# Row statistics of a hybrid attention/LRU layer: spread over partitions by two DMAs instead of two products

## The chip, the cores and the metric

The kernel runs on one core of one Trainium2 chip. The metric is the device time of one execution in microseconds (us). In the rows below PE is TensorE (PEld its weight loads), DVE VectorE, ACT ScalarE, POOL GpSimd, and SP the engine that does nothing here but issue DMAs. A name such as `SPq` is an engine's queue of issued instructions.

## The reference

One layer of a trunk over 512 tokens of width 2048: a norm, one input projection, an attention group and a recurrent (LRU) group side by side, a norm and a gate for each group, one output projection.

```python
h = rms_norm(x, norm_w)
proj = jnp.einsum('bsd,de->bse', h, w_in)
q, k, v, g_attn, xr, g_lru = jnp.split(proj, SPLITS, axis=-1)
attn_out = attention_group(q, k, v, q_norm_w, k_norm_w)
lru_out = lru_group(xr, conv_w, conv_b, lru_wa, lru_ba, lru_wx, lru_bx, lru_lambda)
mixed = jnp.concatenate([rms_norm(attn_out, attn_norm_w) * jax.nn.silu(g_attn),
                         rms_norm(lru_out, lru_norm_w) * jax.nn.silu(g_lru)], axis=-1)
return x + jnp.einsum('bse,ed->bsd', mixed, w_out)
```

`rms_norm` divides a token's row by the root of its mean square and multiplies by a weight for each column. Everything is float32.

## The kernel before

**Layout.** Activations are held with features on the 128 partitions and the 512 tokens along the free axis. Each float32 operand of a product is split into a high part in the matmul's input format (fp32r) and a low part, the rest; a product is then three matmuls (`mm3`, L153 to L155). The high part is made on ACT (`wh`, L218), the low part on DVE (`wl`, L219), so every 512 KB chunk of weights passes a DMA (`wr`, L206, a ring of three buffers), two ACT casts and two DVE subtractions before PE can use it.

**The norm's weights.** `norm_w` scales the features of x. It is loaded as 16 rows of 128 (`nw_st`), turned to a column per 128 features by a PE product with the identity (`columns`, L189) and copied to `nw` by DVE (L191). `xturn` (L253 to L261) turns a block of x on PE, scales it by a column of `nw` into the high part (ACT, L258) and the low part (DVE, L261).

**A row's statistic.** The mean square of a token's row is not applied to x, but to what comes out of the projections, where a token is a place on the free axis. So its reciprocal root, computed as one number per token on the partitions (a 128 x 4 tile), must stand on all 128 partitions along the free axis (128 x 512). `rows` does that: it splits the column into high and low part (L354, L355), spreads each over a diagonal matrix of 128 x 512 (L357), multiplies both by a matrix of ones on PE (L363) and copies the result from PSUM (L364). It is used three times: for `rbc`, the statistic of x, in `xstats`; for `gbc`, that of the LRU group, at the end of `kv`; for `gbc` again, that of the attention group, in `later`.

**The stages around the change.** First the LRU input is projected (`proj_feat(C_XR, ...)`, eight chunks of x and weights); its PSUM banks are emptied by DVE with a product by `rbc` (`evac_bc`, L466). Then come the second half of it with the LRU itself, k and v, the two halves of q, and the gates with the attention. `kv` runs beside the projection of q: POOL raises the LRU group's mean squares to the power of -0.5 (`rsqrt_mean`, L343 and L344, tile `r_l`), four fill steps later `rows` makes `gbc`, and `normed` (L826) multiplies the four pairs of LRU outputs `hs` by it on DVE. When q's second half is done, ACT empties its banks (L591), and `norm_rope` normalises and rotates it on DVE (L608 to L617) with statistics `rr` from POOL. The first head's q, which went through DRAM to be turned (`put_aside`, `bring_back`, tiles `qd` and `lq`, L289 and L296), is split into parts by ACT and DVE (L648) and enters the first product with k.

**What sets the order.** PE runs in the order in which the program is written. ACT, DVE and POOL are ordered by a scheduler from priorities, except at the very start and at the end. SP's issues are in written order during the first projection and in the attention, and the scheduler's between. Each engine runs its own list strictly in order: an instruction that waits holds up all behind it. SP and ACT issue DMAs into queues over the same 16 DMA engines; each of these DMAs takes one of eight semaphores in turn, and waits for the landing of the DMA that had it before. POOL also issues DMAs that add rows of `w_out` into DRAM (`t`, L897).

`moves` is a table that says at which step of the first projection a chunk's next stage is written: `x5` is the next stage of x's chunk 5 (load, turn in 32 x 32 blocks, put aside in DRAM, bring back, split), `w5` and `s5` load and split the weights of chunk 5.

Of the kernel before, what the change touches and what calls it, by code (L numbers as in the profile page):

```python
# [17 lines left out]
P = 128  # L18
# [21 lines left out]
SOON = 150  # L40


WARM, WARM2 = 11, 5


BEGIN, STEPS, LATE = 11, 2, 3
# [17 lines left out]
def hybrid_kernel(  # L64
# [53 lines left out]
    def nm(s):  # L118
        cnt[0] += 1
        return f"{s}_{cnt[0]}"  # L120
# [4 lines left out]
    def k2(dt=F32, shape=(P, SEQ)):  # L125
        return pools["lru"].tile(list(shape), dt, tag="k2", bufs=LRU_K2, name=nm("k2"))
# [19 lines left out]
    def const(shape, name, dt=F32):  # L146
        return cp.tile(list(shape), dt, tag=name, name=name)

    def f(ap):
        return ap.bitcast(F32)  # L150
# [29 lines left out]
            nc.sync.dma_start(vec_st[lo : lo + src.shape[0], :], src)  # L180

    nw = const([P, KT], "nw")
    vec = const([P, R_END], "vec")

    def columns(dst, src):

        n = src.shape[0]
        pt = mm()
        nc.tensor.transpose(pt[:, :n], src, ident[:n, :n])  # L189
        with tc.high_priority():  # L190
            nc.vector.tensor_copy(dst, pt[:, :n])  # L191
# [8 lines left out]
    def wraw(w, r0, c0, nk=1, queue=nc.sync):  # L200

        raw = wring.tile([P, 2, SEQ], F32, name=nm("wr"))
        src = w[r0 : r0 + 2 * P, c0 : c0 + SEQ].rearrange("(k p) e -> p k e", p=P)
        for k in range(nk):
            ks = slice(k * 2 // nk, (k + 1) * 2 // nk)
            loads_done[queue] = queue.dma_start(raw[:, ks, :], src[:, ks, :]).ins  # L206
            yield raw
# [26 lines left out]
    def xload(c, nk=1):  # L234

        xc = b4(shape=(P, NT, 2 * P))
        for k in range(nk):
            ks = slice(k * 2 * P // nk, (k + 1) * 2 * P // nk)
            cs = slice(c * 2 * P + ks.start, c * 2 * P + ks.stop)
            nc.sync.dma_start(xc[:, :, ks], xf[:, cs].rearrange("(t p) d -> p t d", p=P))  # L240
            yield xc
# [7 lines left out]
    def xturn(xc, kk, then=None):  # L249
        pt = mm()  # L250
        for t in range(NT):
            ks = slice(kk % 2 * P, (kk % 2 + 1) * P)
            nc.tensor.transpose(pt[:, t * P : (t + 1) * P], xc[:, t, ks], ident)  # L253
        if then:
            then()
        xh[kk], xl[kk] = x2(), x2()
        with behind(split_done[-1] if kk > 3 else ()):
            highs[kk // 2] = nc.scalar.activation(  # L258
                xh[kk], pt, AF.Identity, scale=nw[:, kk : kk + 1]
            ).ins  # L260
        nc.vector.scalar_tensor_tensor(  # L261
            xl[kk], pt, nw[:, kk : kk + 1], f(xh[kk]), op0=ALU.mult, op1=ALU.subtract
        )

    def xsquare(xc, c):
# [83 lines left out]
    def rows(dst, col, dg):  # L349

        shape = [P, NT, P]
        part = [const([P, NT], nm("part")) for _ in range(2)]
        parts = [dg() for _ in part]
        nc.vector.tensor_copy(part[0].bitcast(F32R), col)  # L354
        nc.vector.tensor_sub(part[1], col, part[0])  # L355
        for c, d in zip(part, parts):
            nc.vector.tensor_mul(  # L357
                d, ident[:, None, :].broadcast_to(shape), c[:, :, None].broadcast_to(shape)
            )
        pb = mm()  # L360
        for k, d in enumerate(parts):
            d = d.rearrange("p t q -> p (t q)")
            nc.tensor.matmul(pb, ones_r, d, start=k == 0, stop=k == 1)  # L363
        nc.vector.tensor_copy(dst, pb)  # L364

    def xstats():
        s = const([P, NT], "xsum")
        nc.vector.reduce_sum(s, ssq, axis=AX.X)
        rsqrt_mean(rstd, s, DM, NT)
        rows(rbc, rstd, lambda: k2(F32R, (P, NT, P)))  # L370

# [278 lines left out]
    def kv(es):  # L650
        turned_k = sent(norm_rope(es, NKV, rk), NKV)
        yield 20
        opened("wx", "right")
        for t in range(NT):
            vv = es[t][:, NKV * HD :]
            vt = aside(
                lambda *a: pools["qkv"].tile(*a, tag="v", bufs=NT, name=nm("v")), 2 * NKV * HD // H
            )
            vh[t], vl[t] = vt[:, 0, :], vt[:, 1, :]
            nc.scalar.copy(vh[t], vv)  # L660
            nc.vector.tensor_sub(vl[t], vv, f(vh[t]))
        yield from lru_squares()
        yield 2
        drain(turned_k)
        yield 6
        pair = landed(asides.pop(0))
        for h in range(NKV):
            yield (12, 4)[h]
            kt = pools["qkv"].tile([P, 2, SEQ], F32R, tag="kt", bufs=NKV, name=nm("kt"))
            kth[h], ktl[h] = kt[:, 0, :], kt[:, 1, :]  # L670
            split_head(pair, h, kth[h], ktl[h])
        r = group_rstd(sums["l"], "r_l", NB * P)
        yield 4
        rows(
            gbc, r,
            lambda: pools["rope"].tile([P, NT, P], F32R, tag="kv", bufs=NT, name=nm("kv")),
        )

    qs = {}

# [468 lines left out]
    given = {}  # L1149
    with tc.high_priority():  # L1150
        xs, ws = xload(0, 2), wraw(w_in, 0, C_XR, 2)
        nc.scalar.dma_start(nw_st, norm_w.rearrange("(k p) -> k p", p=P))
        xc, raw = next(xs), next(ws)
        next(xs), next(ws)
        table = const([P, 1], "table")
        nc.scalar.activation(table, ones[:, :1], AF.Exp)
        first = []

        def scales():
            columns(nw, nw_st)  # L1160
            first.append(wsplit(raw, 0, nc.vector.tensor_copy))

        xturn(xc, 0, scales)
        busy(WARM2)
    chunks = [xchunk(c) for c in range(1, KT // 2)]

    raws = {}
# [5 lines left out]
    def split_x(c):  # L1173
# [10 lines left out]
    }  # L1184

    def move(step):
        for name in moves.get(step, "").split():
            n = int(name[1])
            if name[0] == "x":
                next(chunks[n - 1])  # L1190
            else:
                (fetch_x if name[0] == "w" else split_x)(n)

    for step in proj_feat(C_XR, a1, first, given):
        if step is None:
            with tc.high_priority():
                first.append(wsplit(raw, 1))
                xturn(xc, 1)
            xsquare(xc, 0)
            move(None)  # L1200
            given[1] = wload(w_in, 2 * P, C_XR)
            continue
        c, e = step
        move(step)
        if (c, e) == (1, 2):
            s2.close()
        if (c, e) == (4, 2):
            with tc.high_priority(AHEAD):
                vec_load()
        if (c, e) == (7, 1):  # L1210
            columns(vec, vec_st)
        if (c, e) == (KT // 2 - 1, 0):
            with tc.high_priority(), tc.issue_after(x_parts[1]):
                xstats()

    s1.close()
    last_x = loads_done["lru"] = loads_done[nc.sync]
# [213 lines left out]
```

## Time and profile before

| | us |
|---|---|
| time, median of 3 runs | 631.48 (631.18 to 632.32) |
| the profiled execution's own time | 631.68 |
| its span, first to last instruction | 629.9 |
| PE busy in the span | 624.1 (99%) |
| DVE busy | 491.5 (78%) |
| ACT busy | 348.3 (55%) |
| POOL busy | 103.6 (16%) |

Times in rows are from the span's start. What lies outside the span is 1.8 us of the profiled execution. PE is busy almost throughout, so what changes the time is what PE executes, and the places where it waits for another engine's result.

### The profile page before, as it was taken

The numbers are of one execution on the slowest core, as the hardware profiler recorded it, in microseconds if no ns is written. First come the engines' busy times: TensorE is split into PE (matmuls) and PEld (weight loads), VectorE is DVE, ScalarE is ACT, GpSimd is POOL, SyncE is SP. The second block draws the span as 40 slices with busy tenths as digits, with TensorE's granted clock in tenths as the row PEclk, the third lists the DMA queues.
The fourth block names the chain that finished last, engine by engine and source line by source line (L and its number), as shares of the span: only waits on it lengthen the run. The fifth ranks groups of instructions, "written<-read, shape, count | busy, mean of one in ns | idle before, by whom it ended". The sixth has DMA issues, their size and how long they took to land.

```text
span 629.9 us, 8298 instructions
## 1 busy us (share of the span) xinstructions
PE 624.1 (99%) x2768; PEld 514.0 (82%) x2768; DVE 491.5 (78%) x796; ACT 348.3 (55%) x612; POOL 103.6 (16%) x137
## 2 busy tenths in 40 slices
PE   9999999999999999999999999999999999999997
PEld 7887888888888888888888888888888888888885
DVE  5948879986699874887887888549978866886875
ACT  3764799479945812555475447435445633444441
POOL 0001110112003631622122232100300001010010
PEclk9999999999999999999999999999999999999999
DMA  9878785859784599479669646923995677896262
GB/s 292 279 208 248 185 206 148 183 138 199 232 233 135 170 250 232 99 208 270 186 175 250 201 146 188 267 69 129 254 223 187 210 253 237 293 330 223 68 200 100
DMA packets 73594, 127.61 MB, mean 203 GB/s; under 512 B 6616, under 2 KB 29264, under 8 KB 73552
## 3 DMA queue, kind: packets, MB, share of 16 engines
q1 hardware_dynamic: 65664, 109.65, 56.4%
q0 software_dynamic: 7712, 17.31, 14.3%
q8 instruction: 21, 0.34, 0.2%
q14 instruction: 21, 0.17, 0.1%
q10 hardware_dynamic: 176, 0.14, 0.1%
HBM read 110.29 MB, written 37.75 MB: 235 GB/s over the span
## 4 chain that ended last, share of the span: by engine, by line
PE 95%; DMA 2%; DVE 1%; SPq 1%; ACT 0%; issue 0%; POOL 0%; DVEq 0%; ACTq 0%; POOLq 0%
PE pj L153 19%; PE pj L155 19%; PE pj L154 19%; PE mm L1021 14%; PE pj L1021 10%; PE mm L155 4%; PE mm L153 3%; PE mm L154 3%; PE pj L383 1%; DMA xd<-xu 1%; DMA xu<-xd 1%; PE mm L253 1%; PE mm L1139 1%; SPq L296 0%; DVE xu L281 0%
## 5 line engine op out<-in xcount | busy, mean ns | idle before, releaser
L153 PE MATMUL pj<-x,wh 128*128 128x512 f32 x376 | 146.9, 391 | 0.0
L154 PE MATMUL pj<-x,wh 128*128 128x512 f32 x376 | 146.5, 390 | 0.0
L155 PE MATMUL pj<-x,wl 128*128 128x512 f32 x376 | 146.5, 390 | 0.0
L218 ACT CAST wh<-wr 128x512 fp32r<-128x512 f32 x143 | 85.7, 618 | 93.0 <-PE pj L154 36.3
L219 DVE TENSOR_TENSOR wl<-wr,wh 128x512 fp32r<-128x512 f32 x144 | 100.2, 723 | 18.7 <-ACT wh L218 17.5
L873 ACT CAST wh<-wr 128x1024 fp32r<-128x1024 f32 (+1 forms) x72 | 60.7, 860 | 75.0 <-PE mm L1021 35.4
L874 DVE TENSOR_TENSOR wl<-wr,wh 128x1024 fp32r<-128x1024 f32 (+1 forms) x72 | 68.7, 985 | 29.7 <-ACT wh L873 29.6
L155 PEld LDWEIGHTS pj<-x,wl 128*128 128x128 f32 x376 | 70.6, 188 | 15.2 <-DVE wl L219 0.3
L154 PEld LDWEIGHTS pj<-x,wh 128*128 128x128 f32 x376 | 70.6, 188 | 14.6
L153 PEld LDWEIGHTS pj<-x,wh 128*128 128x128 f32 x376 | 70.6, 188 | 14.6
L153 PE MATMUL pj<-wh,x 128*128 128x512 f32 x192 | 74.8, 390 | 0.0
L155 PE MATMUL pj<-wh,x 128*128 128x512 f32 x192 | 74.7, 389 | 0.0
L154 PE MATMUL pj<-wl,x 128*128 128x512 f32 x192 | 74.7, 389 | 0.0
L897 POOL DMA_DIRECT2D t<-in_w_out_dram x40 | 33.7, 914 | 131.7 <-DMA t<-in_w_out_dram 88.4
L1021 PE MATMUL mm<-wl,mh 128*128 128x512 f32 x128 | 49.8, 389 | 0.0
L1021 PE MATMUL mm<-wh,mh 128*128 128x512 f32 x128 | 49.8, 389 | 0.0
L1021 PE MATMUL mm<-wh,ml 128*128 128x512 f32 x128 | 49.8, 389 | 0.0
L154 PEld LDWEIGHTS pj<-wl,x 128*128 128x128 f32 x192 | 36.0, 188 | 7.5
L153 PEld LDWEIGHTS pj<-wh,x 128*128 128x128 f32 x192 | 36.0, 188 | 7.5
L155 PEld LDWEIGHTS pj<-wh,x 128*128 128x128 f32 x192 | 36.0, 188 | 7.5
L703 POOL TENSOR_SCALAR p<-p,sm 128x512 f32<-128x512 f32 x32 | 23.7, 744 | 89.8 <-DVE sm L702 89.8
L1021 PE MATMUL pj<-wl,mh 128*128 128x512 f32 x96 | 37.4, 390 | 0.0
(209 smaller groups left out, 1035.5 us busy)
## 6 DMA issues: line engine op xcount, KB each, us to landing
wr<-in_w_in_dram SPq DMA_DIRECT2D x71, 512.0 KB, 5.1
wr<-in_w_out_dram SPq DMA_DIRECT2D x24, 512.0 KB, 5.2
t<-in_w_out_dram POOLq DMA_DIRECT2D x40, 256.0 KB, 7.0
wr<-t SPq DMA_DIRECT2D x40, 256.0 KB, 6.0
pd<-u SPq DMA_DIRECT2D x16, 512.0 KB, 3.0
pt<-pd SPq DMA_DIRECT2D x64, 128.0 KB, 3.8
t<-in_w_out_dram SPq DMA_DIRECT2D x24, 256.0 KB, 5.3
t<-t SPq DMA_DIRECT2D x16, 256.0 KB, 5.2
```

What stands on the lines that cost most here:

```text
L153: nc.tensor.matmul(acc, lh, rh, start=start, stop=False)
L154: nc.tensor.matmul(acc, lh, rl, start=False, stop=False)
L155: nc.tensor.matmul(acc, ll, rh, start=False, stop=stop)
L218: copy(hi, raw[:, k, :]).ins,
L219: nc.vector.tensor_sub(lo, raw[:, k, :], f(hi)).ins,
L253: nc.tensor.transpose(pt[:, t * P : (t + 1) * P], xc[:, t, ks], ident)
L383: nc.tensor.matmul(acc[e], w[:, e * P : (e + 1) * P], x_[k], start=k == 0 and j == 0, stop=False,)
L703: last_pool[0] = nc.gpsimd.tensor_scalar(p, p, sm, 0.0, op0=ALU.mult, op1=ALU.add).ins
L873: nc.scalar.copy(hi[:, to], b)
L874: nc.vector.tensor_sub(lo[:, to], b, f(hi[:, to]))
L897: nc.gpsimd.dma_start(dst, src, accum_op=ALU.add)
L1021: nc.tensor.matmul(dst[s], lh[:, ts_], rh, start=i == 0 and j == 0, stop=i == 7 and j == 2)
```

## The change

`spread` takes the place of `rows` for `rbc` and for the LRU group's `gbc`: SP writes the 128 x 4 column to 512 consecutive floats in DRAM (`line`), waits until that has landed, and reads them back to all 128 partitions at once. The attention group keeps `rows`. `xstats` becomes a generator with two stages, written at two places of the `moves` table (`t0`), in place of a call behind the last split of x. The first two columns of the norm's weights are fetched by a DMA of their own, issued by ACT, straight into `nw0`; the turn of all 16 columns stays, but is written behind the second block of x. Of the small products that keep PE busy while it waits for the first data (`busy`), the second batch is three instead of five.

```diff
-WARM, WARM2 = 11, 5
+WARM, WARM2 = 11, 3
...
+    nw0 = const([P, 2], "nw0")
+
+    def scale_of(kk):
+        return (nw if kk > 1 else nw0)[:, kk : kk + 1]
...
-                xh[kk], pt, AF.Identity, scale=nw[:, kk : kk + 1]
+                xh[kk], pt, AF.Identity, scale=scale_of(kk)
...
-            xl[kk], pt, nw[:, kk : kk + 1], f(xh[kk]), op0=ALU.mult, op1=ALU.subtract
+            xl[kk], pt, scale_of(kk), f(xh[kk]), op0=ALU.mult, op1=ALU.subtract
...
+    def spread(dst, col):
+
+        line = dram.tile([SEQ], F32, name=nm("line"), tag="line", bufs=2)
+        nc.sync.dma_start(line.rearrange("(t p) -> p t", p=P), col)
+        yield
+        nc.sync.dma_start(dst, line[None, :].broadcast_to([P, SEQ]))
+        yield
+
     def xstats():
         s = const([P, NT], "xsum")
         nc.vector.reduce_sum(s, ssq, axis=AX.X)
         rsqrt_mean(rstd, s, DM, NT)
-        rows(rbc, rstd, lambda: k2(F32R, (P, NT, P)))
+        yield from spread(rbc, rstd)
...
         r = group_rstd(sums["l"], "r_l", NB * P)
         yield 4
-        rows(
-            gbc, r,
-            lambda: pools["rope"].tile([P, NT, P], F32R, tag="kv", bufs=NT, name=nm("kv")),
-        )
+        drain(spread(gbc, r))
...
+        nc.scalar.dma_start(nw0, norm_w[: 2 * P].rearrange("(k p) -> p k", p=P))
         nc.scalar.dma_start(nw_st, norm_w.rearrange("(k p) -> k p", p=P))
...
-        def scales():
-            columns(nw, nw_st)
-            first.append(wsplit(raw, 0, nc.vector.tensor_copy))
-
-        xturn(xc, 0, scales)
+        xturn(xc, 0, lambda: first.append(wsplit(raw, 0, nc.vector.tensor_copy)))
         busy(WARM2)
+    stats = xstats()
...
-        (4, 0): "x6 w7 x7", (4, 3): "s5 x6",
+        (4, 0): "x6 t0 w7 x7 t0", (4, 3): "s5 x6",
...
+            elif name[0] == "t":
+                with tc.high_priority(AHEAD):
+                    next(stats)
...
                 xturn(xc, 1)
+                columns(nw, nw_st)
...
-        if (c, e) == (KT // 2 - 1, 0):
-            with tc.high_priority(), tc.issue_after(x_parts[1]):
-                xstats()
```

How the built programs stand, at the three places that matter. The first is SP's list in the first projection, where chunk 6 of x is brought back (`xu`), the weights of chunk 7 are loaded and chunk 7 is brought back; the two `xd` ahead are the writes that put them aside. Before:

```order
L289 DMA xd_437<-xu_425 128x1024
L296 DMA xu_420<-xd_431 32x4x256 x4
L206 DMA wr_483<-in_w_in_dram 128x2x512
L296 DMA xu_426<-xd_437 32x4x256 x4
L180 DMA vec_st<-in_conv_w_dram 32x128
```

and with the change:

```order
L294 DMA xd_437<-xu_425 128x1024
L301 DMA xu_420<-xd_431 32x4x256 x4
L374 DMA line_487<-rstd 128x4x1
L211 DMA wr_489<-in_w_in_dram 128x2x512
L301 DMA xu_426<-xd_437 32x4x256 x4
L376 DMA rbc<-line_487 128x512
L180 DMA vec_st<-in_conv_w_dram 32x128
```

The write of the column stands between the two chunks, and the read ahead of the small constants (`vec_st`) and all that follows them.

The second is DVE's list at the LRU group's statistic, with buffer numbers. Each `wl` is the low part of one half of a chunk of weights; `wl_513` and `wl_515` before, `wl_505` and `wl_507` now, are the two halves of the first chunk of the gates. Before:

```order
L819 COPY r_l_2372<-mm_455_2367 128x4
L354 CAST part_461_2411<-r_l_2372 128x4
L355 TENSOR_TENSOR part_462_2412<-r_l_2372,part_461_2411 128x4
L357 TENSOR_TENSOR kv_463_2413<-ident_82,part_461_2411 128x512
L357 TENSOR_TENSOR kv_464_2414<-ident_82,part_462_2412 128x512
L219 TENSOR_TENSOR wl_513_2600<-wr_511_2597,wh_512_2599 128x512
L364 COPY gbc_102<-mm_465_2419 128x512
L826 TENSOR_TENSOR hs_163_884<-hs_163_884,gbc_102 128x1024
L826 TENSOR_TENSOR hs_203_1083<-hs_203_1083,gbc_102 128x1024
L826 TENSOR_TENSOR hs_272_1443<-hs_272_1443,gbc_102 128x1024
L219 TENSOR_TENSOR wl_515_2604<-wr_511_2597,wh_514_2603 128x512
L826 TENSOR_TENSOR hs_321_1696<-hs_321_1696,gbc_102 128x1024
```

and with the change:

```order
L829 COPY r_l_2363<-mm_451_2358 128x4
L224 TENSOR_TENSOR wl_505_2582<-wr_503_2579,wh_504_2581 128x512
L836 TENSOR_TENSOR hs_159_875<-hs_159_875,gbc_103 128x1024
L836 TENSOR_TENSOR hs_199_1074<-hs_199_1074,gbc_103 128x1024
L224 TENSOR_TENSOR wl_507_2586<-wr_503_2579,wh_506_2585 128x512
L836 TENSOR_TENSOR hs_268_1434<-hs_268_1434,gbc_103 128x1024
L836 TENSOR_TENSOR hs_317_1687<-hs_317_1687,gbc_103 128x1024
L224 TENSOR_TENSOR wl_510_2592<-wr_508_2589,wh_509_2591 128x512
L621 TENSOR_TENSOR ev_468_2489<-ev_468_2489,rr_472_2497 128x512
```

The five instructions that made the spread are gone; the first product with `gbc` waits for a DMA now, and stands ahead of the second half of the chunk, of the next chunk and of the rotation of q (`ev`, `rr`).

The third is SP's list at the same place. Before, where `lq_2627` and `lq_2632` are pieces of the first two pairs of q heads coming back:

```order
L296 DMA lq_2627<-qd_2180 32x4x256 x2
L206 DMA wr_2617<-in_w_in_dram 128x2x512
L296 DMA lq_2627<-qd_2180 32x4x256
L296 DMA lq_2632<-qd_2186 32x4x256 x4
L206 DMA wr_2649<-in_w_in_dram 128x2x512
```

and with the change:

```order
L211 DMA wr_2599<-in_w_in_dram 128x2x512
L374 DMA line_2402<-r_l 128x4x1
L301 DMA lq_2609<-qd_2171 32x4x256
L301 DMA lq_2614<-qd_2177 32x4x256
L376 DMA gbc<-line_2402 128x512
L301 DMA lq_2614<-qd_2177 32x4x256 x3
L211 DMA wr_2631<-in_w_in_dram 128x2x512
```

The write goes out behind a 512 KB load of weights, and the read, which must wait for the write's landing, stands ahead of three pieces of q and all later loads of weights.

## The prediction

> **What bounds the kernel now.** I read the page first, for what is busy.
>
> ```profile
> span 629.9 us, 8298 instructions
> PE 624.1 (99%) x2768; PEld 514.0 (82%) x2768; DVE 491.5 (78%) x796; ACT 348.3 (55%) x612; POOL 103.6 (16%) x137
> ```
>
> PE leaves 5.8 us of the span idle. So the time falls only by what PE no longer executes or waits for, and it rises by every wait that PE gets. The next question is what the products of `rows` (L363) cost PE. The timeline of PE around both, columns start and duration in us:
>
> ```profile
> 49.54 0.39 PE L154 MATMUL pj<-x,wh 128*128 128x512 f32 x1
> 49.77 0.39 PE L155 MATMUL pj<-x,wl 128*128 128x512 f32 x1
> 50.15 1.01 PE L363 MATMUL mm<-k,ones_r 128*128 128x512 f32 x2
> 51.00 0.40 PE L153 MATMUL pj<-x,wh 128*128 128x512 f32 x1
> ...
> 238.23 0.39 PE L155 MATMUL pj<-wh,x 128*128 128x512 f32 x1
> 238.46 0.62 PE L363 MATMUL mm<-kv,ones_r 128*128 128x512 f32 x2
> 238.91 0.40 PE L153 MATMUL pj<-wh,x 128*128 128x512 f32 x1
> ```
>
> Matmuls overlap, so a price is read from start to start: 0.23 us from one to the next in a dense stretch (49.54 to 49.77). Without the two products of `rbc` the matmul of 51.00 would start at 50.00, so they cost 1.00 us, of which 0.46 is work and the rest waiting for DVE's diagonals. The two of `gbc` cost 238.91 - 238.23 - 0.23 = 0.45 us, without a wait.
>
> **The change, part by part. The products.** Both pairs go: -1.00 and -0.45 us. The gain holds only if the DMAs that replace them deliver before anyone needs the result. That is two questions, one for each place.
>
> **rbc.** The squares of x, from which `rbc` comes, are done long before it is used, and the new order starts from there.
>
> ```profile
> 31.73 0.08 DVE L272 DVE_READ_ACCUMULATOR b<-b 128x1 f32 x1
> 33.98 1.74 SPq L296 DMA_DIRECT2D xu<-xd  x4
> 35.81 0.40 SPq L206 DMA_DIRECT2D wr<-in_w_in_dram  x1
> 43.30 4.58 SPq L206 DMA_DIRECT2D wr<-in_w_in_dram  x3
> 52.86 1.92 DVE L466 TENSOR_TENSOR ev<-pj,rbc 128x512 f32<-128x512 f32 x3
> 50.52 1.29 DVE L219 TENSOR_TENSOR wl<-wr,wh 128x512 fp32r<-128x512 f32 x2
> 55.27 0.39 PE L153 MATMUL pj<-x,wh 128*128 128x512 f32 x1
> wr<-in_w_in_dram SPq DMA_DIRECT2D x1, 512.0 KB, 5.9
> ```
>
> The last square ends at 31.8. The sum and POOL's two steps need some 1.6 us (the root of the other statistic, quoted below, takes 1.03 alone), so the column is ready about 33.5, before SP has issued the four `xu` at 35.7: the write waits for nothing. The 512 KB load next to it took 5.9 us (last row, issued at 35.81), so I take up to 6 for the write, and as much for the read: `rbc` at about 47 or 48, and its first use cannot come before the first bank is complete at 50. Behind the waiting read stand SP's small constants and the load that went out at 43.30. They start when the write has landed, by 42 instead of behind the row of 35.81 and four more `xu`, so that load comes at most some 4 us late; it is split by DVE at 50.52 and wanted by PE at 55.27. I take 0. If SP stood there longer than that difference of some 4.8 us, PE would wait for the rest.
>
> **The start.** Rows of all engines, and the DMA of the first two pieces of x:
>
> ```profile
> 3.62 1.09 PE L253 MATMUL mm<-ident,b 128*128 128x128 f32 x4
> 4.64 0.28 PE L189 MATMUL mm<-ident,nw_st 16*128 16x16 f32 x1
> 4.96 0.17 DVE L191 COPY nw<-mm 128x16 f32<-128x16 f32 x1 [4.96 <-PE mm L189]
> 5.17 0.69 ACT L258 ACTIVATE x<-mm,nw 128x512 fp32r<-128x512 f32 x1 [2.47 <-DVE nw L191]
> 5.91 1.43 PE L383 MATMUL pj<-x,wh 128*128 128x512 f32 x4
> b<-in_x_dram SPq DMA_DIRECT2D x2, 256.0 KB, 2.8
> ```
>
> ACT waits for `nw`, made from the product at 4.64. With `nw0` it could start when the four turns end, at 4.71: 0.46 earlier at best. The small product moves into the dense part and costs up to its 0.28 there; the two dropped `busy` products filled a wait. The new load is 256 single floats that share the DMA engines with x's first piece, which is in use 0.13 us after landing (0.72 + 2.8 against 3.62); a delay there eats the rest. I take 0, between -0.46 and +0.4.
>
> **gbc** decides. First, how much time it has. DVE's rows from the statistic to q's split, PE's first product with k, PE's first matmul of the gates, and SP's first load behind q's pieces:
>
> ```profile
> 239.84 3.50 DVE L826 TENSOR_TENSOR hs<-hs,gbc 128x1024 f32<-128x1024 f32 x3
> 243.26 0.68 DVE L219 TENSOR_TENSOR wl<-wr,wh 128x512 fp32r<-128x512 f32 x1
> 243.86 1.22 DVE L826 TENSOR_TENSOR hs<-hs,gbc 128x1024 f32<-128x1024 f32 x1
> 253.01 0.69 DVE L608 TENSOR_TENSOR ev<-ev,rr 128x512 f32<-128x512 f32 x1 [5.05 <-POOL rr L344]
> 255.87 0.68 DVE L219 TENSOR_TENSOR wl<-wr,wh 128x512 fp32r<-128x512 f32 x1
> 256.85 0.69 DVE L608 TENSOR_TENSOR ev<-ev,rr 128x512 f32<-128x512 f32 x1 [0.30 <-POOL rr L344]
> 267.21 1.29 DVE L648 TENSOR_TENSOR q<-lq,q 128x512 fp32r<-128x512 f32 x2
> 267.95 0.19 PEld L155 LDWEIGHTS mm<-kt,q 128*128 128x128 f32 x1 [0.27 <-DVE q L648]
> ...
> 252.54 0.39 PE L153 MATMUL pj<-x,wh 128*128 128x512 f32 x1
> 243.97 13.01 SPq L206 DMA_DIRECT2D wr<-in_w_in_dram  x2
> ```
>
> The row of 267.95 is the point: PE's first product with q already waits for DVE's split of q, so this stretch of DVE has no slack at its end. From 256.85 to 267.21 DVE works without a marked wait (10.36 us), from 253.01 to the end of the `wl` 3.46 (to 256.47). Ahead of that now come, from the moment G when `gbc` lands: two `hs` (1.14 each from start to start, 3.42 for three), a `wl` (0.60), two `hs`, a `wl`: 5.76 us. So q is split from G + 5.76 + 3.46 + 10.36 = G + 19.6. It is wanted at 267.21, or 266.75 with PE 0.45 us ahead. `gbc` must land by 247.1, on the clock of this trace; each us later is a us in which PE waits. (The gates start at 252.54; the half chunk behind the first two `hs` is wanted five matmuls later, about 253.3 with the 0.45, and is ready at G + 3.0: hurt only from G = 250.3, later than q.) No DVE time saved in the spread helps, since DVE waited 5.05 us at 253.01 for POOL anyway. The four `hs` were hidden in that wait.
>
> Now when it lands. POOL's root, and the DMAs around it: one `wr` issued at 233.28, one `lq` at 233.91, the packets of both queues from 241 to 245, a `t` issued at 244.4, and the load of all engines over the stretch (its DMA share is the second figure from the end).
>
> ```profile
> 233.60 1.03 POOL L344 TENSOR_TENSOR r_l<-r_l,nhalf 128x4 f32<-128x4 f32 x1
> wr<-in_w_in_dram SPq DMA_DIRECT2D x1, 512.0 KB, 10.2
> lq<-qd SPq DMA_DIRECT2D x1, 128.0 KB, 11.3
> ...
> q0 software_dynamic: 316, 0.58, 79.2%
> q1 hardware_dynamic: 328, 0.33, 31.4%
> ...
> t<-in_w_out_dram POOLq DMA_DIRECT2D x1, 256.0 KB, 7.3
> ...
> 235.00:250.00 15.00, 15.00 (x67) 12.39 (x67) 8.46 (x11) 3.09 (x7) 3.85 (x5) 1.00 1.10 247
> ```
>
> The DMA engines are full from 235 to 250 (share 1.10). The column is ready at 234.6, and its write is issued then, right behind the `wr` that landed at 243.5; an `lq` in nearly that place took 11.3 us and landed at 245.2, though it is a quarter of the size. The small write cannot pass what is queued ahead of it: 243.5 is the lower bound. Its 512 floats go to places that are not neighbours to what a partition holds; if each is a piece of its own against the 128 rows of an `lq`, then at 328 packets in 4 us, in turn with as many of POOL's, 512 take 6.2 us from 243.5: 249.7 is the upper bound. POOL has fewer left by then, so I take 246.0. The read is issued at once, and SP's queue is nearly empty, since SP stood still: 2.8 us (the piece of x of the same size) to 7.3 (POOL's `t`, same size, same time). I take 3.8, nearer the lower. G = 249.8, with ends 246.3 and 257.0; PE waits 2.7 us, with ends 0 and 9.9. Behind SP's wait stand three pieces of q for later heads and the loads that began to go out at 243.97. The first of them is the gates' fourth chunk, wanted three chunks of 24 matmuls (5.5 us each) behind 252.54, about 269: issued even 9 us later, at 253, and 10.2 us on its way, it is there at 263.
>
> By the Trainium skill's page "DMA: Bandwidth & Descriptors", section "Anatomy of one DMA — SWDGE (gpsimd) path" (it is fitted on POOL's DMAs), a DMA costs about 2.0 us and its bytes at 436 per ns; by that both together would take 4.6 us, `gbc` would land near 239.3 and nothing would wait. The 2.8 us of x in an empty queue agrees with it; the 10.2 and 11.3 here do not.
>
> **The sum**, against the profiled execution (631.68, span 629.9): -1.00 - 0.45 + 0 + 0 + 2.7 = +1.25 us, so 632.9 there; that execution is 0.2 above the median, 631.48, which becomes **632.7**. 1.26 us is 0.2%, about what a measurement of this kernel tells from no change.
>
> **The rivals.**
> 1. *`gbc` lands in time, faster.* If the write and the read take under 12.5 us together, the products' price is won: 631.48 - 1.45 = 630.0. For it: the lower ends (246.3), the 2.8 us of x; the page's rule above gives the same. Against it: the `wr` ahead, which by its 10.2 us leaves the pair of DMAs only 3.6 us behind its own landing. It decides from G = 247.1.
> 2. *Both trips as slow as the slowest neighbours.* G = 257.0, PE waits 9.9 us: 631.5 - 1.45 + 9.9 = 639.9. Against it: POOL's queue runs dry at some time, and SP adds nothing while it waits.
> 3. *The start loses.* The 256 single floats delay the first pieces by more than the wait that they remove: +0.4 on the case that holds otherwise, 630.4 in time and 633.1 as forecast.
>
> **How the numbers follow.** Forecast, G between 248.5 and 253: 0.55, with 631.4 to 635.9 as its own range. Rival 1, G below 248.5: 0.28, where two thirds lie below 247.3 and so beyond 0.2%. Rival 2: 0.10. Rival 3 beside a `gbc` in time: 0.07, mostly within 0.2%. Faster: 0.19 + 0.02 = 0.21. Within 0.2%: 0.09 of rival 1, 0.13 of the forecast (G up to 249.8 is its early part), 0.04 of rival 3: 0.26. Slower: 0.53. The range runs from 629.9, where rival 1's cluster lies, to 636.5; some 0.1 lies above, as much at and under the lower end.
>
> **What would show it.** In the changed kernel's trace: no L363 products at 50 and 238 and no gap there; DVE waiting at its first `hs` for a DMA, until about 249 to 250; the write of `line` landing some 10 us or more after its issue at about 233.6; PE waiting near 267 for DVE's split of q; the first matmul of the projection within 0.4 us of 5.91. The forecast is wrong if DVE's wait ends before 247, or if it ends at 250 and PE still does not wait for q, or if PE waits for `vec`, `rbc` or a chunk of weights before 60.

## The result, and the profile after

The changed kernel takes **655.7 us** (median of six runs, 651.4 to 658.8) against 631.48: a ratio of 1.0376, with an interval of 1.0332 to 1.0421. It is 24 us slower, where 1.2 us had been forecast. The profiled execution took 658.77 us. Its page, in the parts that answer to those of before (busy time, the granted clock in 40 slices, the chain that ended last, the two groups of PE with idle time ahead of them):

```profile
span 657.0 us, 8286 instructions
PE 635.8 (97%) x2762; PEld 517.4 (79%) x2762; DVE 488.3 (74%) x786; ACT 348.1 (53%) x612; POOL 102.9 (16%) x137
PEclk9997999999999999799999999999999999999999
PE 87%; DMA 7%; DVE 3%; ACT 1%; issue 1%; SPq 0%; POOL 0%; DVEq 0%; ACTq 0%; POOLq 0%
L155 PE MATMUL pj<-x,wl 128*128 128x512 f32 x376 | 149.0, 396 | 7.8 <-DVE wl L224 7.8
L153 PE MATMUL pj<-x,wh 128*128 128x512 f32 x376 | 148.7, 395 | 5.6 <-ACT wh L223 5.6
```

PE is busy for 635.8 us, 11.7 longer than before, although it executes six products less, and idle for 21.2 instead of 5.8. So waits are 15.4 us of the 27.1 that the span has grown, and in the rest the products themselves became slower. The clock was granted in part in two slices, the fourth (49 to 66 us) and the seventeenth (263 to 279). To place the loss I number the matmuls of the projections, the scores and the output, which are the same in both traces, and compare their starts (us; lag is after less before):

| matmul | before | after | lag | between |
|---|---|---|---|---|
| 1st | 5.91 | 6.28 | 0.4 | |
| 16th | 10.17 | 12.50 | 2.3 | start |
| 168th | 48.41 | 50.57 | 2.2 | |
| 169th | 48.64 | 56.55 | 7.9 | wait for chunk 7 |
| 201st | 57.08 | 66.46 | 9.4 | half clock, less the products of `rbc` |
| 961st | 229.35 | 240.54 | 11.2 | no gap anywhere |
| 997th | 238.91 | 249.82 | 10.9 | products of `gbc` gone |
| 1062nd | 253.67 | 272.96 | 19.3 | wait for a half chunk |
| 1125th | 267.96 | 290.23 | 22.3 | half clock, wait for q |
| last | 624.86 | 651.78 | 26.9 | no gap anywhere |

PE waits for chunk 7 because ACT's cast of its weights stands behind ACT's work on the last pieces of x (`xu`), for which ACT waited 12.9 us.

PE's timeline at the two waits, and at q (columns start and duration in us; in brackets the idle time ahead and what ended it):

```profile
50.57 0.39 PE L155 MATMUL pj<-x,wl 128*128 128x512 f32 x1
56.55 0.79 PE L153 MATMUL pj<-x,wh 128*128 128x512 f32 x1 [5.59 <-ACT wh L223]
...
61.45 0.49 PE L155 MATMUL pj<-x,wl 128*128 128x512 f32 x1
...
264.73 0.40 PE L154 MATMUL pj<-x,wh 128*128 128x512 f32 x1
272.96 0.80 PE L155 MATMUL pj<-x,wl 128*128 128x512 f32 x1 [7.84 <-DVE wl L224]
...
276.55 0.46 PE L154 MATMUL pj<-x,wh 128*128 128x512 f32 x1
...
290.23 0.50 PE L155 MATMUL mm<-kt,q 128*128 128x512 f32 x1 [0.95 <-DVE q L661]
```

A wait costs more than its length. From 56.55 to 61.45 there are 11 matmuls from start to start, 0.45 us each instead of 0.23: another 2.4 us. From 272.96 to 276.55 there are eight: 1.8 us. All engines in these two stretches; the third figure from the end is the granted clock, half of full:

```profile
56.50:61.50 5.00, 4.95 (x12) 3.69 (x13) 2.18 (x4) 2.17 (x4) 0.00 (x0) 0.50 0.98 294
...
273.00:276.50 3.50, 3.50 (x8) 2.77 (x9) 3.46 (x5) 0.00 (x0) 0.00 (x0) 0.50 0.51 150
```

By the Trainium skill's page "TensorE: Matmul & The Clock Gate", section "Part 1: The HAM clock gate", PE drops to half its clock after an idle window of about 3.4 us and needs a busy one to come back; both waits here, 5.59 and 7.84, agree, and the 0.95 for q has no such tail.

DVE's row at the second wait shows what held it:

```profile
269.95 2.36 DVE L836 TENSOR_TENSOR hs<-hs,gbc 128x1024 f32<-128x1024 f32 x2 [22.08 <-DMA gbc<-line]
```

What made both late are the DMAs. SP's issues at the first place, then the DMA rows (sizes, us from issue to landing) of the DMAs issued from 36 to 47 us and from 244 to 263.7, then the busy time of all engines in three stretches (the last three figures are the granted clock, the DMA engines' share and the GB/s that they moved):

```profile
35.68 0.38 SPq L374 DMA_DIRECT2D line<-rstd  x1
36.16 0.45 SPq L211 DMA_DIRECT2D wr<-in_w_in_dram  x1
45.93 0.34 SPq L376 DMA_DIRECT2D rbc<-line  x1
```
```profile
wr<-in_w_in_dram SPq DMA_DIRECT2D x1, 512.0 KB, 15.0
xu<-xd SPq DMA_DIRECT2D x4, 128.0 KB, 15.3
rbc<-line SPq DMA_DIRECT2D x1, 256.0 KB, 8.2
```
```profile
t<-in_w_out_dram POOLq DMA_DIRECT2D x5, 256.0 KB, 15.0
gbc<-line SPq DMA_DIRECT2D x1, 256.0 KB, 6.3
line<-r_l SPq DMA_DIRECT2D x1, 2.0 KB, 17.6
```
```profile
36.00:47.00 11.00, 11.00 (x50) 9.09 (x50) 4.26 (x7) 4.20 (x8) 0.00 (x0) 1.00 0.32 26
...
245.00:252.00 7.00, 7.00 (x32) 5.64 (x31) 0.69 (x1) 0.62 (x1) 3.47 (x4) 1.00 1.16 252
252.00:263.00 11.00, 11.00 (x49) 8.89 (x48) 0.00 (x0) 4.27 (x13) 1.15 (x2) 1.00 1.15 73
```

The write of 2 KB kept SP 10.25 us (35.68 to 45.93) and 17.6 us at the second place. While it is under way, everything else on all queues crawls: the load of weights behind the first write took 15.0 us where the one in its place took 5.9 before, and POOL's `t`, on another queue, 15.0 instead of 7.3. From 252 to 263 the DMA engines are as busy as in the seven us ahead (1.15 against 1.16) and move 73 GB/s instead of 252. The first 4 us of the 17.6 are the queue: most of the write's pieces pass between 250 and 252 us (482 packets under 512 bytes there, 26 from 246 to 248), and the crawl begins behind them.

### The profile page after: what moved, and what is told of

It reads as the page before. It is cut to its first block, busy times and chain, and to the rows that moved or that the text cites. A ratio compares the mean times of both kernels' runs of the same rounds, so it can differ in the third digit from the quotient of the medians.

```text
span 657.0 us, 8286 instructions
## 1 busy us (share of the span) xinstructions
PE 635.8 (97%) x2762; PEld 517.4 (79%) x2762; DVE 488.3 (74%) x786; ACT 348.1 (53%) x612; POOL 102.9 (16%) x137
## 4 chain that ended last, share of the span: by engine, by line
PE 87%; DMA 7%; DVE 3%; ACT 1%; issue 1%; SPq 0%; POOL 0%; DVEq 0%; ACTq 0%; POOLq 0%
PE pj L154 17%; PE pj L153 17%; PE pj L155 17%; PE mm L1031 13%; PE pj L1031 10%; PE mm L155 3%; PE mm L154 3%; PE mm L153 3%; DMA line<-r_l 3%; DMA xu<-xd 2%; PE pj L396 1%; DMA gbc<-line 1%; PE mm L258 1%; DVE wl L224 1%; ACT b L273 1%
## 5 line engine op out<-in xcount | busy, mean ns | idle before, releaser
L155 PE MATMUL pj<-x,wl 128*128 128x512 f32 x376 | 149.0, 396 | 7.8 <-DVE wl L224 7.8
L153 PE MATMUL pj<-x,wh 128*128 128x512 f32 x376 | 148.7, 395 | 5.6 <-ACT wh L223 5.6
L154 PE MATMUL pj<-x,wh 128*128 128x512 f32 x376 | 148.6, 395 | 0.0
L224 DVE TENSOR_TENSOR wl<-wr,wh 128x512 fp32r<-128x512 f32 x144 | 100.2, 724 | 22.3 <-ACT wh L223 21.3
L153 PEld LDWEIGHTS pj<-x,wh 128*128 128x128 f32 x376 | 71.6, 190 | 21.6 <-ACT wh L223 6.0
L154 PEld LDWEIGHTS pj<-x,wh 128*128 128x128 f32 x376 | 71.6, 190 | 15.9
```

The lines of the kernel that those rows point to most:

```text
L153: nc.tensor.matmul(acc, lh, rh, start=start, stop=False)
L154: nc.tensor.matmul(acc, lh, rl, start=False, stop=False)
L155: nc.tensor.matmul(acc, ll, rh, start=False, stop=stop)
L224: nc.vector.tensor_sub(lo, raw[:, k, :], f(hi)).ins,
```

## The experiments

Each stands against runs of the kernel before, taken beside it.

**The parts alone.** Three kernels with one part of the change each, and a fourth with both spreads, in which PE turns the column ahead of the write (against the changed kernel's `spread`; besides, `rbc` is written one step later in the `moves` table, and `gbc` two fill steps earlier):

```diff
+        pt = mm()
+        nc.tensor.transpose(pt[:NT, :P], col, ident)
+        row = const([NT, P], nm("row"))
+        with tc.high_priority():
+            nc.vector.tensor_copy(row, pt[:NT, :P])
...
-        nc.sync.dma_start(line.rearrange("(t p) -> p t", p=P), col)
+        nc.sync.dma_start(line.rearrange("(t p) -> t p", p=P), row)
```

> The kernel before with only the start of the change (two columns of the norm's weights fetched as 256 single floats, the small product moved, three filling products instead of five). Theory, that the loss of the change is the sum of three separate places: PE's first turn waits for x's piece 0.8 us longer and the clock is granted full later, +2.3 us, 633.8. Rival, that the start is harmless (the prediction's 0, between -0.46 and +0.4) and its lag in the changed kernel's trace is made up later: 631.0 to 631.9.

> The kernel before with only rbc spread by the write and the broadcast read, at the places of the changed kernel. Theory, that the write of 512 single floats itself holds up all DMA queues: the write takes about 10 us, the four xu and the wr behind it about 15, PE stands some 6 us near 51 and runs at half clock after it: 638 to 639. Rival, that x's stage was late there only because the start was late: the xu take 5 to 7 us, PE does not stand, 630.5.

> The kernel before with only the LRU group's gbc spread by the write and the broadcast read. Theory, that the write of single floats holds up all queues: the write lands 15 us or more after its issue at 234, gbc near 258 to 260, PE stands some 8 us at the second half chunk of the gates and restarts at half clock: 641 to 643. Rival, the prediction's own account of the queues, without the start and rbc ahead of it: gbc at 249.8, PE waits 2.7 us for q, 633.7.

> The kernel before with both spreads by write and read, but the column first turned by one small product with the identity to 4 x 128 and copied by DVE, so that the write is four rows of 512 B instead of 512 single floats; start as before. Theory, that the single floats are what holds up the queues: the write takes 2 to 4 us at the first place and no longer than its neighbours (10 to 12 us) at the second, nothing else gets slower, 630.3 to 633.5. Rival, that it is the two trips through DRAM with SP waiting between them, whatever the pieces: as slow as the two spreads of single floats, about 650.

| | us | before beside it | ratio (interval) |
|---|---|---|---|
| start alone | 639.18 | 632.99 | 1.0110 (1.0085 to 1.0135) |
| `rbc` alone | 643.64 | 632.99 | 1.0176 (1.0145 to 1.0207) |
| `gbc` alone | 646.24 | 632.99 | 1.0220 (1.0172 to 1.0269) |
| both, turned | 635.98 | 632.99 | 1.0058 (1.0036 to 1.0079) |

All four lie above what their theories gave at most, by 5.4, 4.6, 3.2 and 2.5 us. The first three lose 6, 11 and 13 us, 30 together, more than the 24 of the whole: something is counted more than once. The traces of `rbc` alone and of `gbc` alone show the same slow write without the other parts (9.3 us at the first place, 18.1 at the second). In the list of waits (waited for by whom, us in total, times, longest) the rows of `gbc` alone are

```profile
DVE hs L831 <- DMA gbc<-line: 22.9, 1, 22.9
...
PE pj L155 <- DVE wl L219: 8.7, 1, 8.7
```

which is the changed kernel's wait again. The turned column removes it: its writes took 2.8 and 5.9 us. But in all four traces PE also loses 4 to 6 us between 65 us and the end without a gap, the start-only kernel nearly all of its 6.2 there, where nothing was changed.

**The loss without a gap.** A smaller list of constants or a new one moves every buffer that is allocated behind them. `nw0` takes 32 bytes of each partition, a `part` of `rows` 32, a `row` 512. So the ring of weights and all behind it stand 96 bytes lower in the changed kernel, 32 higher with the start alone, 64 lower with one spread, 896 higher with both turned. Four kernels: before itself; before with a constant that nobody uses; the start with `nw0` placed in a constant that is filled later; the turned spreads with their rows in `nw_st` and the freed bytes held.

```diff
+    const([P, 2], "shift")
     vec = const([P, R_END], "vec")
```

> The kernel before itself, profiled beside the others. In all four experiments so far PE's matmuls drifted apart from about 65 us on, where nothing was changed: the usual 227 ns from start to start became 230 to 236, 4 to 5.5 us by the end. If this comes from the chip of the moment, this run shows it too: 631 to 634 with the same drift in its trace. If the changes bring it, this run's trace agrees with the first one of before within 0.5 us from 65 us to the end.

> The kernel before with an unused constant of 8 bytes per partition, allocated where the change allocates the two columns of the norm's weights. It moves the buffers of weights, x and the packed outputs by 32 bytes, from multiples of 64 to odd multiples of 32, and changes nothing else. Theory, that the place in memory makes the drift: 3 to 6 us slower than before, spread evenly, no single gap. Rival, that places do not matter: within 0.5 us of before.

> The start of the change alone, as in the first experiment, but with the two columns kept in the first two columns of a constant that is filled later, so that no buffer moves. Theory, that the start costs 0.4 to 1 us and the rest of that experiment's 6.2 us was the place of the buffers: 0.4 to 1.2 us slower than before beside it. Rival, that the start itself costs it all: 6 us slower again.

> Both spreads with the column turned first and written as four rows of 512 B, as in the fourth experiment, but the rows kept in a constant that is no longer needed and the freed bytes held, so that every buffer in the fast memory stands where it stands before (scratch in DRAM still moves by 4 KB). Theory, that the fourth experiment's 3 us came from moved buffers: -1.0 - 0.45 + 0.9 for q, -0.5 us against before. Rival, that they come from the spreads: +3 us again.

Before against itself is 631.9 to 632.18, 0.9996 (0.9984 to 1.0009), and its PE drifts by 0.7 us from 65 us to the end, a little more than the 0.5 allowed for: it is not the chip. The unused constant costs 5.9 us (638.12 to 632.18, 1.0086, 1.0063 to 1.0108). The start with its buffers in place costs 0.8 us (1.0009, 0.9998 to 1.0019) instead of 6.2. The turned spreads, 635.21 to 632.18 (1.0060, 1.0035 to 1.0085), miss the -0.5 of their theory and come out at the rival's +3: their drift is gone, but PE waits 1.63 us for a half chunk and 1.78 us for q, since DVE's wait for `gbc` ended at 251.6:

```profile
251.60 2.36 DVE L837 TENSOR_TENSOR hs<-hs,gbc 128x1024 f32<-128x1024 f32 x2 [8.96 <-DMA gbc<-line]
...
260.34 0.50 PE L155 MATMUL pj<-x,wl 128*128 128x512 f32 x1 [1.63 <-DVE wl L219]
271.28 0.50 PE L155 MATMUL mm<-kt,q 128*128 128x512 f32 x1 [1.78 <-DVE q L662]
```

Then the same unused constant with 256, 512 and 2048 bytes.

> The kernel before with an unused constant of 256 bytes per partition: the same buffers as in the 32-byte experiment move, by 256. If the drift depends on a place modulo 64, 128 or 256, there is none here (within 0.5 us of before); else 3 to 6 us slower.

> As the one before, moved by 512 bytes. If the drift depends on a place modulo 512, there is none here (within 0.5 us of before); else 3 to 6 us slower.

> As the one before, moved by 2048 bytes. If the drift depends on a place modulo 1024 or 2048, there is none here (within 0.5 us of before); if it depends on the distance to the buffers that did not move, 3 to 6 us slower.

None of them costs anything: 1.0002 (0.9992 to 1.0012), 0.9995 (0.9984 to 1.0007) and 1.0004 (0.9994 to 1.0013). How many matmuls PE executed from 480 to 620 us (PE's count is in the first brackets), in before itself, with 32 bytes, with 256, and in the fully changed kernel of the next experiment:

```profile
480.00:620.00 140.00, 139.94 (x618) 115.50 (x617) 110.19 (x136) 62.00 (x77) 11.43 (x18) 1.00 0.66 214
```
```profile
480.00:620.00 140.00, 140.00 (x608) 113.71 (x607) 108.16 (x135) 62.41 (x78) 11.44 (x18) 1.00 0.66 215
```
```profile
480.00:620.00 140.00, 140.00 (x619) 115.90 (x618) 110.43 (x137) 62.39 (x77) 11.44 (x18) 1.00 0.65 214
```
```profile
480.00:620.00 140.00, 140.00 (x619) 115.87 (x618) 108.73 (x135) 63.10 (x78) 10.15 (x16) 1.00 0.70 225
```

PE is busy throughout at full clock in all four; with the 32 bytes it gets ten matmuls less done in 140 us, 230 ns each instead of 227. The loss is not everywhere: from 400 to 470 us both kernels get 313 done. Moves by multiples of 256 bytes were free; moves by 32, -64, -96 and 896 (128 beyond a multiple of 256) were not, the second and the last by the drift in their traces alone. Why the place matters is open. The trace gives no sign that another engine is in the way: of the matmuls from 480 to 620 us with the 32 bytes, those with DVE at work throughout take 230.8 ns from start to start and those with DVE idle 231.4; for ACT it is 231.3 and 230.5.

**The whole change with its buffers in place.**

> The whole change, with every buffer in the fast memory put back where it stands before (the two columns kept in a constant filled later, the freed bytes held). Theory, that 6 us of the change's 24.2 us come from the buffers moved by 32 bytes: 17 to 19 us slower than before beside it, and in the trace no drift between the three places. Rival, that the moved buffers cost nothing beside the waits of the changed kernel: 23 to 25 us.

652.27 to 632.2, 1.0297 (1.0262 to 1.0332): 20.1 us by the medians and 18.8 by the ratio, where the change has 24.2 and 23.7. In its trace the lag behind before itself does not grow from the wait for q to the end: 21.2 us at 270 us and at 600. The theory's 17 to 19 holds by the ratio and not by the medians. So the moved buffers account for some 4 to 5 us, a rough figure, since the runs of the two kernels spread over 6 and 7 us; the rest lies at the three places. They vary: in this trace the second write took 22.3 us and PE waited 13.0 us behind it, 7.8 in the first. Its wait at the first place, 3.1 us, a little short of the page's 3.4, was followed by the half clock too (granted 0.55 from 55 to 58 us).

**What makes the write slow.** A kernel before with a chain of DMAs behind its end; each write of the same 512 floats waits for the one ahead.

```diff
+        "side": (side.rearrange("(t p) -> p t", p=P), rstd, wide(side)),
+        "packed": (packed.rearrange("(p t) -> p t", t=NT), rstd, wide(packed)),
+        "apart": (apart[:, :, 0], rstd, (rbc[:, :NT], apart[:, :, 0])),
+        "full": (full, nw_st[:NT, :], wide(full.rearrange("t p -> (t p)"))),
```

In each line stand the place in DRAM, what is written, and the read behind it (`wide` is the broadcast read). `side` is the layout of the change, `packed` has 16 bytes of each partition together, `apart` single floats 512 bytes apart, `full` four rows of 512 bytes.

> The kernel before with a chain of DMAs behind its end, one after another, so the time itself says nothing (100 to 200 us more). Each writes a column of 512 floats to DRAM, alone or with a 512 KB load of weights right behind, in four layouts: as in the change (neighbouring places from neighbouring partitions), 16 bytes per partition, single floats 512 bytes apart, four full rows. Theory 1, that single floats are slow as pieces: both single layouts take 8 us or more alone and make the load behind them 10 us late, the other two 2 to 3 us and nothing. Theory 2, that it is the neighbouring places written from many engines at once: only the layout of the change is slow, singles 512 bytes apart take 3 to 4 us. Theory 3, that it takes the load of the real place: all four take 2 to 4 us here.

SP's issues. The read behind each write is issued when the write has landed, so the time from one row to the next is the write's:

```profile
630.80 0.38 SPq L1408 DMA_DIRECT2D side<-rstd  x1
639.73 0.33 SPq L1412 DMA_DIRECT2D rbc<-side  x1
644.94 0.33 SPq L1408 DMA_DIRECT2D packed<-rstd  x1
647.25 0.32 SPq L1412 DMA_DIRECT2D rbc<-packed  x1
650.65 0.60 SPq L1408 DMA_DIRECT2D apart<-rstd  x1
653.10 0.58 SPq L1412 DMA_DIRECT2D rbc<-apart  x1
656.12 0.28 SPq L1408 DMA_DIRECT2D full<-nw_st  x1
657.92 0.34 SPq L1412 DMA_DIRECT2D rbc<-full  x1
...
677.03 0.36 SPq L1408 DMA_DIRECT2D side<-rstd  x1
677.44 0.50 SPq L206 DMA_DIRECT2D wr<-in_w_in_dram  x1
686.72 0.33 SPq L1412 DMA_DIRECT2D rbc<-side  x1
```

On idle queues the layout of the change takes 8.9 us (10.9 in a repeat, 9.7 with the load behind it); 16 bytes per partition take 2.3, the rows 1.8, and single floats 512 bytes apart 2.5 (2.9, 1.2 and 2.8 with the load). The last is what decides between the theories. Packets of the two, each with the busy share of the DMA engines, in tenths, in 40 slices of the stretch from issue to landing (630.7 to 639.7 us, 650.6 to 653.0):

```profile
DMA  0000370000000000000000000000000000000000
DMA packets 528, 0.00 MB, mean 0 GB/s; under 512 B 528, under 2 KB 528, under 8 KB 528
...
DMA  0000000000000000000000687783000000000000
DMA packets 528, 0.00 MB, mean 1 GB/s; under 512 B 528, under 2 KB 528, under 8 KB 528
```

First stands the change's layout, then the one apart: as many pieces of the same size, and a quarter of the time. In both the pieces pass within half a us. What differs is the time from the last piece to the landing, 7.6 us against 0.8, in which no packet moves. So it is not the count of the pieces, nor their passing, but something behind them that comes with neighbouring four-byte places. What that is was not tried, nor whether it matters that the neighbours come from different partitions, nor from what distance on it ends. The last three rows above have a load of 512 KB right behind the change's write. The packets from 677 to 686.7, when the write landed, and the same load alone, at 626:

```profile
DMA packets 628, 0.21 MB, mean 21 GB/s; under 512 B 528, under 2 KB 528, under 8 KB 628
...
wr<-in_w_in_dram SPq DMA_DIRECT2D x1, 512.0 KB, 4.7
```

Alone it was there after 4.7 us; behind the write 0.21 MB had moved in 9.7. Behind the 16 bytes per partition the load took 6.1.

**Versions without it.** `rbc` through turned rows, with all buffers in place; the same with `gbc` too, issued by ACT, three fill steps earlier than in the change; and `rbc` through 16 bytes per partition, with the order mended by a copy on DVE:

```diff
+        nc.sync.dma_start(line.rearrange("(p t) -> p t", t=NT), col)
...
+        nc.sync.dma_start(gbc, line[None, :].broadcast_to([P, SEQ]))
+        nc.vector.tensor_copy(
+            dst.rearrange("q (t p) -> q t p", p=P), gbc.rearrange("q (p t) -> q t p", t=NT)
+        )
```

> The kernel before with only rbc spread through DRAM, its column first turned to four rows of 512 B, and all buffers in their places. Theory: the products' 1.0 us is won and nothing is lost there, as the trace of the second turned experiment has it up to 230 us: 0.7 to 1.1 us faster than before. Rival, that something later gives it back: within 0.3 us.

> As the one before, and the LRU group's gbc too through turned rows, but issued by ACT instead of SP, so that it is not queued behind SP's loads. Theory, that gbc was late in the turned experiments by SP's queue alone: it lands by 245, PE waits for nothing more, 1.2 to 1.6 us faster than before. Rival, that ACT, which must wait for the write's landing before it issues the read, holds up its casts of weights: PE waits 2 us or more near 255, 1 us slower than before or worse.

> The kernel before with only rbc spread through DRAM, without PE: each partition writes its four floats to 16 neighbouring bytes, the read spreads them to all partitions, and a copy on DVE puts them into the order of the tokens. Buffers in their places. Theory, that only places shared between partitions are slow to write: the write takes 2 to 4 us in the real place too, xu and wr behind it 4 to 6, PE does not stand, 0.7 to 1.2 us faster than before. Rival, that 4 floats per partition are small pieces all the same: the write takes 8 us or more and the kernel is 3 us slower or worse.

| | us | before beside it | ratio (interval) |
|---|---|---|---|
| `rbc` turned | 631.51 | 632.20 | 0.9992 (0.9982 to 1.0001) |
| and `gbc` by ACT | 631.94 | 632.20 | 0.9997 (0.9984 to 1.0011) |
| `rbc` packed | 631.56 | 632.44 | 0.9988 (0.9978 to 0.9999) |

The packed one is 0.8 us faster than before (0.1 to 1.4), the only one of all whose interval is below 1, and that by a hair: among so many intervals one such can be chance. SP's issues and DVE's copy in it:

```profile
34.17 0.38 SPq L369 DMA_DIRECT2D line<-rstd  x1
...
38.19 0.34 SPq L372 DMA_DIRECT2D gbc<-line  x1
...
44.58 0.63 DVE L373 COPY rbc<-gbc 128x512 f32<-128x512 f32 x1 [3.18 <-DMA gbc<-line]
```

In the real place, among the same loads, the write took 4.0 us where the change's took 10.25 (9.3 with `rbc` alone). The `wr` and the `xu` behind it took 7.4, more than the 4 to 6 expected, and PE did not wait for them. `gbc` by ACT met neither account: ACT's wait for the write delayed the weights that PE wanted by only 0.2 us, yet `gbc` landed only at 246.8, the read alone 6.8 us (issued at 239.97), and PE waited 0.7 us for q:

```profile
239.97 0.36 ACTq L377 DMA_DIRECT2D gbc<-line  x1
...
246.82 3.50 DVE L837 TENSOR_TENSOR hs<-hs,gbc 128x1024 f32<-128x1024 f32 x3 [10.19 <-DMA gbc<-line]
```

## Why the prediction was wrong

**The products: right.** Both pairs are gone, and the 0.45 us of `gbc` were won (lag 11.37 to 10.91). The 1.00 us of `rbc` cannot be read between two waits in the changed kernel; `rbc` packed gained 1.03 there (its lag behind the trace of before falls from 0.44 to -0.59).

**`rbc`, "up to 6 for the write ... I take 0": this step failed first.** The bound came from the nearest row in the queue, a load of 512 KB in full rows. The write took 10.25 us, and what it did to the others was not in the step at all. The condition that it named, SP standing longer than 4.8 us, was met, but it was not what hurt: the `wr` and the `xu` that PE waited for had been issued within 3 us of the write and lay 15 us in the queues. With PE's wait at 56.55 for a chunk of weights, a sign that the text had named for a wrong forecast came true. Place: +7.2 us.

**The start, "0, between -0.46 and +0.4".** The first matmul came 0.36 us later, within the bounds, because x's first piece landed after 3.6 us, as the 256 single floats did after 3.4. What was left out is that PE's pace at the start is half, and doubles later than before: the lag is 2.3 us by the 16th matmul. The four turns of x's second block stand 0.11 us apart at 7.2 us before, and 0.21 at 8.2 now, where the products around them are 0.43 apart instead of 0.23. That this is the clock is inferred from the doubled times alone; the granted clock reads 1.00 there in both traces. With its buffers in place the start alone costs 0.8 us (interval from -0.1 to 1.2). How much of it the two dropped filling products cost was not tried.

**`gbc`, "I take 246.0" with 249.7 as the upper bound: the step that cost most.** The count of the pieces was right, 512, and priced as if each were like any other packet; the write landed at 263.55. What followed from G was right: with `gbc` at 269.92 the half chunk was to be ready at G + 3.0, 272.9, and came at 272.96; q was to be split at G + 19.6, 289.5, and entered at 290.23. The order of the two reversed because G had passed 250.3, as the text said it would. With the slow write removed and SP's queue kept, the turned spreads had `gbc` at 251.6 against the forecast's 249.8, and cost 3.4 us of waits against 2.7: the two trips took 15.0 us together, from an issue at 236.58, against the forecast's 15.2. That sum is part luck: the write took 9.0 instead of 11.4, the read 6.1 instead of 3.8. So with the slow write gone the account of SP's queue comes near, and the step that failed is the price of 512 neighbouring floats. That the forecast said slower was right, and by its own path, DVE's wait for `gbc` that reaches PE; the size was not. Place: +10.9 us.

The Trainium skill's page "DMA: Bandwidth & Descriptors", section "Rules for kernel authors", says that a last dimension that is not contiguous becomes one descriptor per element. The traces agree on the count, 528 packets for 512 floats. The count does not give the cost: it was 8.9 us or 2.5 us for the same one. The same page's fit of 2.0 us and the bytes at 436 per ns (section "Anatomy of one DMA — SWDGE (gpsimd) path", for POOL's DMAs), which the prediction named beside its first rival, comes near the three other layouts here (1.8 to 2.5 us) and misses the change's by 7.

**What no step had: the moved buffers, 4 to 7 us.** They are 4 to 5 us by the times with the buffers in place, 6.6 as drift in the changed kernel's trace. The change was read as instructions alone. It also moves the buffers of weights by 96 bytes, and PE loses about 1.5% in the stretches where that matters. The Trainium skill's page "SBUF — State Buffer", section "Who interferes with whom", says that PE never waits on anyone there. The traces do not speak against it, since the lost time does not go with DVE's or ACT's work; the ten matmuls that 32 bytes cost in 140 us show that the place of the buffers can slow PE, and nothing here ties that to another engine.

The sum over the trace: 2.2 (start) + 7.2 (`rbc`) + 2.0 (drift) + 10.9 (`gbc`: 11.0 of waits and half clock and 0.4 of drift, less 0.5 of products) + 4.6 (drift) = 26.9 us, the last matmul's lag, against 27.1 in the spans. Forecast and rivals alike bounded the write by neighbours of another layout; a bound from above has to come from a row of the same kind, or be left open.

## What to carry to other kernels

Spread a column over partitions through DRAM only if what each partition writes is a run of its own: 16 bytes per partition, or whole rows after a turn, cost about 2 us on idle queues here, where neighbouring floats from 128 partitions cost 9 and slowed all queues. When a change adds or drops a small constant, hold its bytes so that the large buffers stay where they are, or move them by a multiple of 256 bytes, and test with an unused constant before a loss is blamed on the change itself. A wait of 3 us or more on PE should be priced with the half clock that followed each of them here, about 2 us more.

## What was not expected of the hardware

- 512 floats written to neighbouring places by 128 partitions: 8.9 to 10.9 us on idle queues, of which the pieces take half a us; 8.4 to 10.3 at the first place in the kernel and 17.6 to 22.3 at the second, some of it spent in the queue. Behind its pieces all queues together moved 73 GB/s instead of 252. The same floats 512 bytes apart: 2.5 us.
- PE at full clock without a gap does 618 matmuls in 140 us with the buffers in one place and 608 with most of them 32 bytes further on; 256, 512 and 2048 bytes change nothing. The loss does not go with the work of DVE or ACT.
